# Holding back two pairs of weight loads with copies of one column

## The chip, the cores and the metric

The kernel runs on one core of a Trainium2 chip. The metric is device time in microseconds (us), the median of the runs of one kernel; lower is better. Engine names are those of the profile: PE is TensorE (PEld its weight loads), DVE is VectorE, ACT is ScalarE, POOL is GpSimd, SP is SyncE, which here only issues DMAs. ACT and POOL issue DMAs too. A name with q (SPq, ACTq, POOLq) is the engine's sequencer.

## The reference

One decoder block on x of 1024 tokens by 1024 channels, all in float32:

```python
h = _rmsnorm(x, g_mix_pre)
u_pool, q, k, v, gates = split(h @ w_in + b_in)
y_pool = _multiscale_pool(u_pool, w_pool, pool_scale)      # windows 2, 4, 8, 16; 4 groups of 128
y_attn = _sliding_window_sink_attention(rotary(q), rotary(k), v, sinks)
g_pool, g_attn = split(sigmoid(gates))
merged = g_pool * (y_pool @ w_branch_pool) + g_attn * (y_attn @ w_branch_attn)
x = x + _rmsnorm(merged @ w_out, g_mix_post)
h2 = _rmsnorm(x, g_mlp_pre)
x = x + _rmsnorm(square(relu(h2 @ w_up)) @ w_down, g_mlp_post)
```

The change concerns w_out alone, more exactly when parts of it are fetched from HBM.

## The kernel before

Every product runs on PE as three passes of a reduced-precision type: each operand is split into a high part (a cast on ACT, line L101) and a low part (a subtraction on DVE, L104), and high times high, high times low and low times high are summed. The big products (gates, w_out, w_up, w_down) use Strassen's scheme with seven block products, so they need sums and differences of quarter blocks as operands. For w_out the quarter blocks are W_Q[a, b], each 512 rows by 512 columns, held as two tiles of 512 KB.

The work goes in stages: attention with the pooled inputs woven in, the gates (`gt`, lines L494 to L535), the two branches, the output product (L1027), then w_up and w_down. The gates end by storing 16 sigmoid tiles z to HBM (L693, issued by ACT, queue ACTq). The change lies in the branches:

- Attention branches 0 to 7 (`branch(w_ba[m], ..., 8, m)`), 24 matmuls each on PE (L428, L430). At every even m, `gate_pair` loads the stored gates of two branches as two tiles `zg[8, m // 2]` (L905, 512 KB each, tiles named g); the branch's weights are loaded (L418, tile st) and split into wh (L101, L104); the result, in two PSUM banks mm, is multiplied into the gates on DVE (L916). There are four such banks, so branch m + 2 may begin only when the products L916 of branch m are done.
- `pool_part(gi)` prepares one group of the pooled mixer during branches 2, 3, 5 and 6, groups 1, 0, 2, 3 in this order. It loads d (L920, SP), adds a bias (ACT, L671), sums over the window by doubling (DVE, L675 and L676, into tiles t), finishes d (L679 to L681) and splits it into yphi (ACT) and yplo (DVE). Tiles d, t and the last z of the gates share four buffers of one pool, tag y: the first d waits until a z store has landed.
- Pooled branches 0 to 7 (`branch(wbp_dram[m], ..., 0, m)`) do the same with the group results and the gates `zg[0, m // 2]`.

Along the way the sums of quarter blocks that the output product wants are made by DMA: `wo_load` loads one block (SP), and `wo_add` adds another one to it while it is read (POOL, a DMA that accumulates, `accum_op`). There are two such tile pairs: `sums` (two ga buffers, in the profile s<-in_w_o_dram) and `s3` (two bc buffers).

```python
    def wo_load(quad, place):
        ts = [place([2, 512]) for _ in range(2)]
        for j, t in enumerate(ts):
            nc.sync.dma_start(t, W_Q[quad][2 * j:2 * j + 2].rearrange("k p n -> p k n"))   # L941
        return ts
...
    for m in range(8):
        branch(w_ba[m], lambda k, hl, th: asp[th][k // 2][hl][:, k % 2, :], 8, m)
        if m == 4:
            sums = wo_load((1, 0), a32)
            wo_add(sums, (1, 1))                                                          # L946
```

`sums` is first read in pooled branch 2 (`split_pairs(sums, x_place)`, tiles wo<-s), then gets block (0, 0) added, later (0, 1). `s3` is read only in the output product. Their place in the code is not their place in time. From the branches on the code is outside of the hand-ordered section; a scheduler orders the instructions of each engine, and a load whose buffer is free early is put early. Each engine, and SP's and POOL's queue of DMA issues, then works strictly in its order: an instruction that waits holds up all behind it.

Of the kernel before, what the change touches and what calls it, by code (L numbers as in the profile page):

```python
# [50 lines left out]
def block_kernel(ctx: ExitStack, tc, xt, x, consts, vecs, sinks, b_qkv, g_post, g_mlp_post,  # L51
                 w_qkv, w_u, w_g, w_pool, w_bp, w_ba, w_o, w_up, w_dn, x1_dram, spill, y_dram, wbp_dram, f_dram, out):
    nc = tc.nc
    act, dve, pool, pe = nc.scalar, nc.vector, nc.gpsimd, nc.tensor
# [32 lines left out]
    def bank(tag, shape=None):  # L87
        return psum["pool"].tile([P] + (shape or [512]), F32, tag=tag, name=nm(tag), bufs=psum["bufs"][tag])
# [327 lines left out]
    def load_w(src, shape):  # L416
        ws = stage(shape)
        nc.sync.dma_start(ws, src)  # L418
        hi, lo = wslot(shape), wslot(shape)
        split(hi, lo, ws)  # L420
        return hi, lo

    def mm_fm(bs, whi, wlo, rhs, nk):

        for k in range(nk):
            for th in range(2):
                for hl in range(2):
                    pe.matmul(bs[th], whi[:, k, :], rhs(k, hl, th), start=k == 0 and hl == 0, stop=False)  # L428
            for th in range(2):
                pe.matmul(bs[th], wlo[:, k, :], rhs(k, 0, th), start=False, stop=k == nk - 1)  # L430
# [469 lines left out]
    zg = {}  # L900

    def gate_pair(base, j):
        zg[base, j] = [g32([2, 512]) for _ in range(2)]
        for th, t in enumerate(zg[base, j]):
            nc.sync.dma_start(t, z_dram[base + 2 * j:base + 2 * j + 2, :, th * 512:(th + 1) * 512]  # L905
                              .rearrange("m p n -> p m n"))

    def branch(w, rhs, base, m):
        if m % 2 == 0:
            gate_pair(base, m // 2)  # L910
        z = zg[base, m // 2]
        whi, wlo = load_w(w, [4, P])
        bs = [bank("mm"), bank("mm")]
        mm_fm(bs, whi, wlo, rhs, 4)
        for th in range(2):
            dve.tensor_tensor(z[th][:, m % 2], z[th][:, m % 2], bs[th], ALU.mult)  # L916

    def pool_part(gi):
        u = yy.tile([P, S], F32, tag="y", name=nm("d"))
        nc.sync.dma_start(u, u_dram[gi])  # L920
        for _ in pool_in(gi, u, y_place):
            pass
        hi = xp.tile([P, S], F32R, tag="x", name=nm("yphi"))
        lo = xp.tile([P, S], F32R, tag="x", name=nm("yplo"))
        split(hi, lo, u)
        ysp[gi] = hi, lo
# [3 lines left out]
    def split_pairs(srcs, place):  # L930
        ops = [(place([2, 512]), place([2, 512])) for _ in srcs]
        for (hi, lo), t in zip(ops, srcs):
            split(hi, lo, t)
        return ops

    W_Q = {(a, b): w_o[4 * b:4 * b + 4, :, 512 * a:512 * a + 512] for a in range(2) for b in range(2)}

    def wo_load(quad, place):
        ts = [place([2, 512]) for _ in range(2)]
        for j, t in enumerate(ts):  # L940
            nc.sync.dma_start(t, W_Q[quad][2 * j:2 * j + 2].rearrange("k p n -> p k n"))  # L941
        return ts

    def wo_add(ts, quad):
        for j, t in enumerate(ts):
            pool.dma_start(t, W_Q[quad][2 * j:2 * j + 2].rearrange("k p n -> p k n"), accum_op=ALU.add)  # L946
# [8 lines left out]
    for m in range(8):  # L955
        branch(w_ba[m], lambda k, hl, th: asp[th][k // 2][hl][:, k % 2, :], 8, m)
        if m == 4:
            sums = wo_load((1, 0), a32)
            wo_add(sums, (1, 1))
        if m in (2, 3, 5, 6):  # L960
            pool_part({2: 1, 3: 0, 5: 2, 6: 3}[m])

    def merge(j):
        for z, zp in zip(zg[8, j], zg.pop((0, j))):
            dve.tensor_tensor(z, z, zp, ALU.add)
# [7 lines left out]
    b11, b12 = merged(0, 1), merged(0, 0)  # L973
    for m in range(8):
        branch(wbp_dram[m], lambda k, hl, th: ysp[k][hl][:, th * 512:(th + 1) * 512], 0, m)
        if m % 2:
            merge(m // 2)
        if m == 0:
            wop[1] = split_pairs(wo_load((0, 0), stage), x_place)
            s3 = wo_load((1, 0), bc32)  # L980
            wo_add(s3, (0, 0))
        elif m == 2:
            wop[5] = split_pairs(sums, x_place)
            wo_add(sums, (0, 0))
        elif m in (4, 6):
            j = m // 2 - 2
            gop.setdefault(1, []).extend(split_pairs(b11[j:j + 1], gr))
            dve.tensor_tensor(b11[j], b11[j], b12[j], ALU.subtract)
# [554 lines left out]
```

## Time and profile before

| what | us |
|---|---|
| median of 3 runs | 1117.25 (1117.24, 1117.25, 1119.76) |
| the profiled execution's own time | 1119.41 |
| its span, first to last instruction | 1117.6 |
| PE busy in the span | 1101.0 |
| DVE, ACT, POOL busy | 807.0, 549.5, 54.9 |
| attention branch 0 begins on PE | 320.50 |
| pooled branch 0 begins on PE | 372.04 |
| output product begins on PE | 415.56 |

A timeline row is: start, duration, engine, line, operation, out<-in, shapes, count, and in brackets the idle time of the engine before it with what ended it. Start times count from the span's start. A row of waits is: who waited, for whom, total us, times, longest. In the profile a tile's buffer numbers are left out.

### The profile page before, as it was taken

Reading aid. Unit: us, or ns where it says so; the run is one execution under the profiler, and the core shown is the slowest. Engines: PE = TensorE matmul, PEld = TensorE weight load, DVE = VectorE, ACT = ScalarE, POOL = GpSimd, SP = SyncE. Lnnn points to the kernel's source line nnn. Section 1 sums busy time; section 2 is a strip of 40 time slices with the busy share of each in tenths; the row PEclk is TensorE's granted clock in tenths of the full one; section 3 lists DMA queues with packets and bytes.
Section 4 is the critical chain, followed back from the end, with each engine's and each line's share of the span. In section 5 each row is a group of like instructions: output and inputs, shape, how many; then the busy total and the mean of one; then the engine's idle time right before and its main releaser. Section 6 shows DMA issues by size and latency. Waiting matters only on the chain.

```text
span 1117.6 us, 13863 instructions
## 1 busy us (share of the span) xinstructions
PE 1101.0 (99%) x5119; PEld 909.8 (81%) x5119; DVE 807.0 (72%) x1174; ACT 549.5 (49%) x917; POOL 54.9 (5%) x101
## 2 busy tenths in 40 slices
PE   9999999999998999999999999999999999999997
PEld 7888788888876888888888888888888888888885
DVE  5478867899747896899988866666548944456596
ACT  7466656445422326677545545454444434344342
POOL 0333221000000000000000000000000000000000
PEclk9999999999999999999999999999999999999999
DMA  9305569456787532481357655435697635335672
GB/s 353 133 11 137 147 152 312 148 188 207 262 248 257 138 95 74 141 287 47 130 209 264 242 188 173 176 125 208 214 362 251 205 96 175 104 97 159 197 251 108
DMA packets 88420, 203.19 MB, mean 182 GB/s; under 512 B 7328, under 2 KB 19744, under 8 KB 88352
## 3 DMA queue, kind: packets, MB, share of 16 engines
q1 hardware_dynamic: 76208, 176.35, 47.1%
q10 hardware_dynamic: 5616, 19.66, 4.5%
q0 software_dynamic: 6528, 6.29, 4.0%
q8 instruction: 40, 0.66, 0.2%
q14 instruction: 28, 0.23, 0.1%
HBM read 146.70 MB, written 55.57 MB: 181 GB/s over the span
## 4 chain that ended last, share of the span: by engine, by line
PE 89%; DVE 4%; DMA 4%; ACT 2%; issue 1%; SPq 0%; DVEq 0%; ACTq 0%
PE mm L494 24%; PE at L494 16%; PE at L1385 14%; PE mm L1385 12%; PE mm L428 4%; PE at L1027 4%; PE mm L1027 3%; PE mm L187 3%; PE mm L584 2%; PE mm L430 2%; DMA spill_dram<-z 1%; PE at L196 1%; PE sc L187 1%; PE at L399 1%; DMA g<-spill_dram 1%; PE sc L335 1%
## 5 line engine op out<-in xcount | busy, mean ns | idle before, releaser
L1385 PE MATMUL at<-ar,wh 128*128 128x512 f32 x744 | 169.9, 389 | 0.3 <-DVE ar L104 0.3
L1385 PEld LDWEIGHTS at<-ar,wh 128*128 128x128 f32 x744 | 139.5, 188 | 30.0 <-DVE ar L104 0.7
L104 DVE TENSOR_TENSOR wh<-raw,wh 128x1024 fp32r<-128x1024 f32 x53 | 64.8, 1223 | 97.6 <-ACT wh L101 97.6
L1385 PE MATMUL mm<-ar,wh 128*128 128x512 f32 x576 | 131.0, 389 | 0.0
L101 ACT CAST wh<-raw 128x1024 fp32r<-128x1024 f32 x53 | 55.8, 1053 | 146.1 <-PE at L1385 65.2
L1385 PEld LDWEIGHTS mm<-ar,wh 128*128 128x128 f32 x576 | 108.1, 188 | 22.4
L101 ACT CAST wh<-st 128x512 fp32r<-128x512 f32 (+1 forms) x97 | 61.5, 645 | 65.3 <-PE at L494 19.9
L104 DVE TENSOR_TENSOR wh<-st,wh 128x512 fp32r<-128x512 f32 (+1 forms) x97 | 68.9, 720 | 25.1 <-ACT wh L101 22.7
L494 PE MATMUL mm<-gr,wh 128*128 128x512 f32 x333 | 80.2, 391 | 0.0
L494 PEld LDWEIGHTS mm<-gr,wh 128*128 128x128 f32 x333 | 62.1, 188 | 12.8
L494 PE MATMUL mm<-T,wx 128*128 128x512 f32 x288 | 67.5, 389 | 0.0
L494 PEld LDWEIGHTS mm<-T,wx 128*128 128x128 f32 x288 | 54.1, 188 | 11.2
L494 PE MATMUL at<-T,wx 128*128 128x512 f32 x252 | 59.1, 389 | 0.0
L494 PEld LDWEIGHTS at<-T,wx 128*128 128x128 f32 x252 | 47.3, 188 | 9.8
L494 PE MATMUL mm<-x,wh 128*128 128x512 f32 x240 | 55.2, 389 | 0.0
L494 PEld LDWEIGHTS mm<-x,wh 128*128 128x128 f32 x240 | 45.0, 188 | 9.4
L104 DVE TENSOR_TENSOR ar<-B,ar 128x1024 fp32r<-128x1024 f32 x37 | 45.1, 1220 | 4.2 <-ACT ar L101 4.0
L584 PE MATMUL mm<-x,wh 128*128 128x512 f32 x192 | 47.8, 396 | 0.0
L101 ACT CAST ar<-B 128x1024 fp32r<-128x1024 f32 x37 | 38.9, 1051 | 6.3 <-DMA B<-in_w_dn_dram 3.4
L584 PEld LDWEIGHTS mm<-x,wh 128*128 128x128 f32 x192 | 35.2, 188 | 7.7
L494 PE MATMUL at<-gr,wh 128*128 128x512 f32 x150 | 36.6, 390 | 0.0
L101 ACT CAST wx<-ws 128x512 fp32r<-128x512 f32 x30 | 18.6, 620 | 33.0 <-DVE ws L470 17.9
(386 smaller groups left out, 2160.5 us busy)
## 6 DMA issues: line engine op xcount, KB each, us to landing
raw<-f_dram SPq DMA_DIRECT2D x53, 512.0 KB, 3.7
f_dram<-g SPq DMA_DIRECT2D x30, 512.0 KB, 3.3
B<-in_w_dn_dram SPq DMA_DIRECT2D x24, 512.0 KB, 6.6
st<-in_w_up_dram SPq DMA_DIRECT2D x20, 512.0 KB, 3.8
st<-in_w_g_dram SPq DMA_DIRECT2D x18, 512.0 KB, 4.3
f_dram<-g ACTq DMA_DIRECT2D x17, 512.0 KB, 2.8
g<-spill_dram SPq DMA_DIRECT2D x16, 512.0 KB, 7.2
raw<-in_w_dn_dram SPq DMA_DIRECT2D x16, 512.0 KB, 4.6
```

The costliest lines, as they stand in the source:

```text
L101: act.copy(hi, src)
L104: eng.tensor_tensor(lo, src, f32(hi), ALU.subtract)
L187: pe.matmul(bq, xs_[k][n // 4][:, xh, n % 4 * P:(n % 4 + 1) * P], wq[k][:, h, :], start=k == 0 and j == 0, stop=k == NK - 1 and j == 2)
L196: pe.matmul(bkv_of(n), xs_[k][n // 4][:, xh, n % 4 * P:(n % 4 + 1) * P], wkv[k // 2][:, h, k % 2, :], start=k == 0 and j == 0 and not (joi ...
L335: pe.matmul(sb[:, kv, i, :nk], qt[r, qx, m * P:(m + 1) * P], kx[r, k0:k0 + nk], start=j == 0, stop=j == 2)
L399: pe.matmul(flat(yb), v[:, kv, :], flat(p[:, 4 * kv:4 * kv + 4]), start=j == 0, stop=j == len(mms) - 1)
L428: pe.matmul(bs[th], whi[:, k, :], rhs(k, hl, th), start=k == 0 and hl == 0, stop=False)
L430: pe.matmul(bs[th], wlo[:, k, :], rhs(k, 0, th), start=False, stop=k == nk - 1)
L494: pe.matmul(b, w[:, wh, kt, :], xo[kt][:, xh, :], start=not after and kt == 0 and j == 0, stop=kt == 3 and j == 2, skip_group_check=after)
L584: pe.matmul(b, (whi, wlo)[h][:, k, :], xr(k, xh, th), start=j == 0, stop=j == len(mms) - 1)
L1027: pe.matmul(bs[t], gop[i][kt // 2][gh][:, kt % 2, t * P:(t + 1) * P], wop[i][kt // 2][wh][:, kt % 2], start=not after and kt == 0 and j == ...
L1385: pe.matmul(bs[t], fo[fh][:, k2, t * P:(t + 1) * P], wo_[wh][:, k2, :], start=not after and s2 == 0 and k2 == 0 and j == 0, stop=s2 == NS ...
```

## The change

`wo_load` may be given a tile `behind`. It then first copies one column of it into each new tile on POOL. The load that overwrites the tile must wait for the copy, and the copy waits for what wrote `behind`: here the product L916 of a branch into its second gate tile. `sums` is held so behind attention branch 4, `s3` behind pooled branch 1, which also moves the code of `s3` by one branch. The copied values are overwritten by the loads.

```diff
-    def wo_load(quad, place):
+    def wo_load(quad, place, behind=None):
         ts = [place([2, 512]) for _ in range(2)]
+        for t in ts if behind else ():
+            pool.tensor_copy(t[:, 0, :1], behind[:, 0, :1])
         for j, t in enumerate(ts):
             nc.sync.dma_start(t, W_Q[quad][2 * j:2 * j + 2].rearrange("k p n -> p k n"))
...
         if m == 4:
-            sums = wo_load((1, 0), a32)
+            sums = wo_load((1, 0), a32, zg[8, 2][1])
             wo_add(sums, (1, 1))
...
         branch(wbp_dram[m], lambda k, hl, th: ysp[k][hl][:, th * 512:(th + 1) * 512], 0, m)
+        if m == 1:
+            s3 = wo_load((1, 0), bc32, zg[0, 0][1])
+            wo_add(s3, (0, 0))
         if m % 2:
             merge(m // 2)
         if m == 0:
             wop[1] = split_pairs(wo_load((0, 0), stage), x_place)
-            s3 = wo_load((1, 0), bc32)
-            wo_add(s3, (0, 0))
```

PE, DVE and ACT keep their instructions in the same order; SP and POOL change. On SP, in the stretch of the attention branches, before (st are branch weights, g stored gates, d the pooled groups; s_528 and s_529 are `sums`, s_574 is the second tile of `s3`, whose first tile stood some 30 rows earlier, among the gates' weights):

```order
L418 DMA st_3261<-in_w_ba_dram 128x512
L941 DMA s_528_3346<-in_w_o_dram 128x2x512
L941 DMA s_529_3347<-in_w_o_dram 128x2x512
L905 DMA g_3207<-spill_dram 128x2x512
L905 DMA g_3208<-spill_dram 128x2x512
L418 DMA st_3312<-in_w_ba_dram 128x512
L920 DMA d_3245<-spill_dram 128x1024
L905 DMA g_3308<-spill_dram 128x2x512
L905 DMA g_3309<-spill_dram 128x2x512
L418 DMA st_3352<-in_w_ba_dram 128x512
L941 DMA s_574_3550<-in_w_o_dram 128x2x512
L920 DMA d_3295<-spill_dram 128x1024
```

The same place on SP after:

```order
L418 DMA st_3261<-in_w_ba_dram 128x512
L905 DMA g_3207<-spill_dram 128x2x512
L905 DMA g_3208<-spill_dram 128x2x512
L418 DMA st_3312<-in_w_ba_dram 128x512
L920 DMA d_3245<-spill_dram 128x1024
L905 DMA g_3308<-spill_dram 128x2x512
L905 DMA g_3309<-spill_dram 128x2x512
L418 DMA st_3354<-in_w_ba_dram 128x512
L920 DMA d_3295<-spill_dram 128x1024
```

The three loads of sums are gone from between the gates and the pooled groups; the rest keeps its order. On SP at the pooled branches, after, `sums` now stands between the two tiles of block (0, 0) (st_3539 and st_3540, loaded at pooled branch 0), ahead of the weights of pooled branch 1 (st_3551):

```order
L418 DMA st_3505<-wbp_dram 128x512
L905 DMA g_3680<-spill_dram 128x2x512
L943 DMA st_3539<-in_w_o_dram 128x2x512
L943 DMA s_528_3346<-in_w_o_dram 128x2x512
L943 DMA s_529_3347<-in_w_o_dram 128x2x512
L943 DMA st_3540<-in_w_o_dram 128x2x512
L418 DMA st_3551<-wbp_dram 128x512
```

Before, the two loads s_528 and s_529 were missing there. `s3` (s_578, s_579) moved likewise, to behind the weights of pooled branch 5 and ahead of those of branches 6 and 7. On POOL, from the last of the attention's issues on, before:

```order
L404 DMA y_dram<-yt_1901 256x1x128 x2
L946 DMA s_573_3549<-in_w_o_dram 128x2x512
L946 DMA s_528_3346<-in_w_o_dram 128x2x512
L946 DMA s_529_3347<-in_w_o_dram 128x2x512
L946 DMA s_574_3550<-in_w_o_dram 128x2x512
```

and after:

```order
L404 DMA y_dram<-yt_1901 256x1x128 x2
L941 COPY s_528_3346<-g_3309 128x1
L941 COPY s_529_3347<-g_3309 128x1
L948 DMA s_528_3346<-in_w_o_dram 128x2x512
L948 DMA s_529_3347<-in_w_o_dram 128x2x512
```

The copies stand ahead of the first additions to `sums`. The second additions to `sums` follow in both; only behind them come, after the change, the copies for `s3` and its two additions, which before stood around the first additions to `sums`; the third additions to `sums` are last in both.

## The prediction

> **What bounds the kernel now.** I read the waits of PE first, then PE's timeline where they fall, then back along the engines to what each wait stood on. PE's waits over the whole run (all others are 1.5 us or less and lie elsewhere):
>
> ```profile
> PE mm L428 <- ACT wh L101: 4.0, 1, 4.0
> PE mm L428 <- DVE g L916: 1.7, 1, 1.7
> ```
>
> Both are in the attention branches. PE's timeline there (rows of one branch's first matmul, but for the fifth), and the clock in a window of 4 us (PE, PEld, DVE, ACT and POOL busy, granted clock, DMA share, GB/s):
>
> ```profile
> 320.50 0.39 PE L428 MATMUL mm<-yahi,wh 128*128 128x512 f32 x1
> 333.22 0.47 PE L428 MATMUL mm<-yahi,wh 128*128 128x512 f32 x1 [1.68 <-DVE g L916]
> 348.50 0.47 PE L428 MATMUL mm<-yahi,wh 128*128 128x512 f32 x1 [4.03 <-ACT wh L101]
> 349.04 0.63 PE L428 MATMUL mm<-yahi,wh 128*128 128x512 f32 x1
> 355.71 0.39 PE L428 MATMUL mm<-yahi,wh 128*128 128x512 f32 x1
> 361.15 0.39 PE L428 MATMUL mm<-yahi,wh 128*128 128x512 f32 x1
> 372.04 0.39 PE L428 MATMUL mm<-yphi,wh 128*128 128x512 f32 x1
> ...
> 348.00:352.00 4.00, 3.50 (x9) 2.65 (x10) 3.97 (x7) 0.47 (x1) 0.00 (x0) 0.65 0.80 293
> ```
>
> A branch that waits for nothing takes 361.15 - 355.71 = 5.44. Branches 0 to 4 took 355.71 - 320.50 = 35.21 instead of 27.20: 8.01 us are lost here. Of these branch 2 (due at 320.50 + 2 x 5.44 = 331.38, begun at 333.22) cost 1.84, branch 4 (due 5.44 + 5.44 after 333.22, so 344.10, begun at 348.50) 4.4 with what branches 2 and 3 ran over, and branch 4 itself 355.71 - 348.50 - 5.44 = 1.77, since its matmuls ran at a granted clock of 0.65.
>
> What the waits stood on, DVE and ACT around them:
>
> ```profile
> 317.77 2.88 PE L494 MATMUL mm<-x,wh 128*128 128x512 f32 x12
> 320.63 1.15 ACT L671 ACTIVATE d<-d,vec 128x1024 f32<-128x1024 f32 x1 [10.46 <-DMA d<-spill_dram]
> 321.81 1.23 DVE L675 TENSOR_TENSOR t<-d 128x1023 f32<-128x1023 f32 x1 [5.87 <-ACT d L671]
> 322.96 0.68 DVE L529 TENSOR_TENSOR z<-z,mm 128x512 f32<-128x512 f32 x1
> 326.12 0.35 ACTq L693 DMA_DIRECT2D spill_dram<-z  x1
> 329.99 1.23 DVE L675 TENSOR_TENSOR t<-t 128x1022 f32<-128x1022 f32 x1 [3.29 <-DMA spill_dram<-z]
> 332.39 1.28 DVE L916 TENSOR_TENSOR g<-g,mm 128x512 f32<-128x512 f32 x2
> 334.26 0.15 DVE L681 TENSOR_TENSOR d<-t,d 128x3 f32<-128x3 f32 x1
> 335.11 0.87 SPq L920 DMA_DIRECT2D d<-spill_dram  x1
> 345.35 1.15 ACT L671 ACTIVATE d<-d,vec 128x1024 f32<-128x1024 f32 x1 [8.29 <-DMA d<-spill_dram]
> 346.53 1.23 DVE L675 TENSOR_TENSOR t<-d 128x1023 f32<-128x1023 f32 x1 [5.51 <-ACT d L671]
> 347.67 1.28 DVE L916 TENSOR_TENSOR g<-g,mm 128x512 f32<-128x512 f32 x2
> ```
>
> DVE sits idle for 5.87 and 5.51 us, because the next instruction in its order belongs to a pooled group whose d is not there, and the products L916 that free PE's banks stand behind it. 332.39 is branch 0's product (PE goes on at 333.22), 347.67 is branch 2's (PE goes on at 348.50; the row names ACT, whose last cast ended there as well, but that cast is of a later branch's weights). So the first cause is two late loads of d. The chain of waits and the DMA view say why they are late:
>
> ```profile
> 307.54 9.18 DMA spill_dram<-z
> 316.79 3.82 DMA d<-spill_dram
> 327.92 5.69 DMA spill_dram<-z
> ...
> DMA to landing us min/median/max: 10.2/10.2/10.2
> ...
> spill_dram<-z ACTq DMA_DIRECT2D x14, 512.0 KB, 3.9
> ```
>
> The first d waits for a z store that took 9.18 where the median of 14 such is 3.9; the d issued at 335.11 took 10.2 (the row of that one issue). What else was moving: the queues between 299 and 343 us (packets, MB, share of 16 engines) with the three accumulating issues, and then those of 308 to 312:
>
> ```profile
> q1 hardware_dynamic: 3445, 7.20, 50.7%
> q0 software_dynamic: 816, 1.57, 20.5%
> s<-in_w_o_dram POOLq DMA_DIRECT2D x3, 512.0 KB, 9.5
> ...
> q0 software_dynamic: 198, 0.40, 60.9%
> q10 hardware_dynamic: 3, 0.01, 0.8%
> ```
>
> Three accumulations of 0.52 MB fill all 16 engines for 0.205 x 44 = 9.0 us, 3.0 each; a plain 0.52 MB on q1 takes 0.507 x 44 x 0.524 / 7.20 = 1.6. In 308 to 312 the accumulation (q0) has 60.9% and ACT's queue (q10), where the z store waits, 0.8%.
>
> **The change part by part.**
>
> 1. It takes three plain loads and three accumulations of sums out of 299 to 343: 3 x 1.6 + 3 x 3.0 = 14 of 44 us of DMA time. The earliest load and accumulation of s3, among the gates, go too; PE waits for nothing there, so nothing comes of it.
>
> 2. The z store of 307.54 then lands after 3.9 (the median; at most 9.18 as now). From 311.4: d 3.8, ACT 1.2, so DVE has its L675 at 316.5 and is done at 317.7, ahead of L529, which PE frees at 317.97 (0.2 after the next group begins at 317.77). L529 comes 5.0 earlier than its 322.96, and with it the store of 326.12, now 321.1. The last store hangs on PE's last gate group (320.5) and comes some 4 earlier, 323.9.
>
> 3. DVE's next L675 waited for the store of 326.12 to land, 3.87 after its issue; now at 321.1 + 3.9 = 325.0, again 5.0 earlier. Branch 0's product then runs from 327.4 to 328.7. PE wants it at 331.38, so the first wait goes, with 2.7 to spare.
>
> 4. L681 ends at 329.3. SP reaches the next d once the last store has landed, at 323.9 + 5.7 = 329.6 at the latest (it took 5.69), so at about 330 instead of 335.11. Its landing lies between 3.8 (the first d) and 10.2; I take 5.5, since two gate loads of 1.6 stand ahead of it and no accumulation. Then 335.5, ACT until 336.7, DVE's L675 until 338, branch 2's product behind it, its first half done at 338.7. PE wants it at 320.50 + 4 x 5.44 = 342.26. Even at 10.2 the half is done at 343.4, and 1.2 of the 4.4 is left. So the second wait goes, and the slow stretch with it.
>
> 5. What is added: four copies on POOL, priced by POOL's nearest row, 0.29 each, and waits. The sums come later, and this is the place to look for a new wait:
>
> ```profile
> 359.60 1.28 DVE L916 TENSOR_TENSOR g<-g,mm 128x512 f32<-128x512 f32 x2
> 374.89 1.05 ACT L101 CAST wo<-s 128x1024 fp32r<-128x1024 f32 x1
> 377.90 1.28 DVE L916 TENSOR_TENSOR g<-g,mm 128x512 f32<-128x512 f32 x2
> L305 POOL COPY vf<-qkv x6: 290/295/444, 40.3 to 94.9; 128x128 f32<-128x128 f32 x6
> st<-in_w_o_dram SPq DMA_DIRECT2D x6, 512.0 KB, 3.8
> DMA to landing us min/median/max: 5.6/5.7/6.1
> ...
> s<-in_w_o_dram SPq DMA_DIRECT2D x3, 512.0 KB, 6.1
> DMA to landing us min/median/max: 10.3/10.3/10.3
> ```
>
> Branch 4's product is the row of 359.60; 8.0 earlier it ends at 352.9, the copies at 353.5. The loads land after 3.8 (the median of the same block's plain loads), 357.8 with the second a little behind. The accumulations land after 5.7 (the row of the four after 356 us, when little else moves; the last two rows are the crowd's, the three loads of sums between 299 and 343 and the first accumulation), and POOL issues the second when the first has landed, so 363.5 and 369.5. ACT casts the second sum at 374.89, now due at 366.9: it waits 2.6 there, until 370.6. Behind it on DVE stand its low part, 1.2, and pooled branch 0's product (377.90), first half done at 372.5. PE wants that at 372.04 - 8.0 + 2 x 5.44 = 374.9. Cost 0, with 2.4 to spare; gone when the pair of accumulations takes 2.4 longer.
>
> 6. On SP, the loads of sums wait for the copies until 353.5. Behind them stand the second tile of block (0, 0) and the weights of pooled branch 1, whose buffers DVE frees about then or later. Cost 0. The loads of s3 wait for copies that stand on POOL behind the second additions (issued after 370.6 and one landing later), so until about 378; behind them on SP are the weights of pooled branches 6 and 7. Branch 6 begins on PE at 364.0 + 6 x 5.44 = 396.7, so its weights have over 15 us. s3 itself is read in the output product, over 40 us later. Cost 0.
>
> The sum: -8.0, so the profiled execution of 1119.41 becomes 1111.4. It stands 2.16 over the median of 1117.25. If that is the price of profiling, the median becomes 1109.2. If its waits or its slow stretch were longer than in the median run, the time without them is 1111.4 for every run. The runs themselves lie 2.5 apart (1117.24 and 1119.76), about the size of the slow stretch, and the rest of the kernel is PE at its pace; so I take a value nearer the second, 1111.0.
>
> The Trainium skill (TensorE: Matmul & The Clock Gate, Part 1: The HAM clock gate) says that an idle stretch of about 3.4 us, counted in windows that run freely, halves PE's clock for a while, and that the outcome varies from run to run. By that rule a remnant of 1.2 would bring no slow stretch, and the three runs may differ by it. The trace agrees: 4.03 idle was followed by a clock of 0.65, 1.68 was not.
>
> **The rivals.**
>
> - B, even sharing. The store was slow because three queues shared the engines, and the accumulation held it up only by its share. A third of the engines would give the store 3 x 1.6 + 2.3 = 7.1 (2.3 is 3.9 less 1.6), half of them 5.5, a gain of 1.6 and not 5.3. Then every step up to branch 0's product comes 1.7 earlier (330.7 to 332.0, about 0.3 of PE's wait left), d goes out at 333.4, lands after 7 (10.2 less one accumulation), and branch 2's product is done at 343.5, 1.2 late. 1111.0 + 1.5 = 1112.5. Against it: 0.8% for q10 beside 60.9% for q0. The Trainium skill (DMA: Bandwidth & Descriptors, Queues, rings and completion order) speaks for it: each DMA engine goes round its queues packet by packet. The rows of 308 to 312 do not look like that.
> - C, late sums, on the other side. The loads and the accumulations of sums take as long as in the crowd: 6.1 and twice 10.3. The second sum lands at 353.5 + 6.1 + 10.3 + 0.3 + 10.3 = 380.5, the product's first half is done 3.0 later, pooled branch 2 waits 8.6 and then runs slowly for 1.8: 1111.0 + 10.4 = 1121.4. It decides when the pair needs over 14 instead of 11.7. Against it: 5.6 to 6.1 for the four accumulations after 356.
> - D, nothing comes of it for the second wait: the gate loads that SP sends in a row make the second d as late as now, and only the first wait goes: 1111.0 + 4.4 + 1.8 = 1117.2, or 2.0 below the median, 1115.2. Against it: accumulations and loads of sums are 14 of the 39 us that the engines were busy between 299 and 343.
>
> **How the numbers follow.** A, as worked out, 0.70, from 1109.2 to 1111.4 with a small remnant; B 0.16; C 0.07; D 0.07. About 0.3%, 3.4 us, is what can be told from no change: faster is under 1113.9. A and nearly all of B are there, 0.84; D and a little of B are the same, 0.09; slower is C, 0.07. The range leaves C and D out and reaches from A's lower end to over B: 1109.0 to 1114.0.
>
> **What would show it.** Right: PE has no wait over 0.5 at L428 and the granted clock stays at 1.00 from 344 to 352; the z store of 307.5 lands within 5, ACT's d L671 comes at about 316 and 336; L916 of branch 0 stands before 329; the span is near 1109.6. Wrong: ACT's wo<-s shows an idle time of over 5 that ends by the DMA of s, with PE waiting at pooled branch 2 (C); DVE's L675 still waits over 3 for ACT's d near 340 (B, D).

## The result, and the profile after

The changed kernel takes 1112.08 us in the median of 6 runs (1110.14 to 1114.83). The kernel before, run beside it, took 1118.71 (1117.24 to 1123.13). The ratio is 0.9938, with a 95% interval of 0.9915 to 0.9961: about 6.9 us faster by the ratio, 6.6 by the medians; the forecast was 6.2, from 1117.25 to 1111.0. The profiled execution took 1114.83 (span 1113.1), against 1119.41 (span 1117.6).

PE's waits in the branches, after (the columns are total, times, longest):

```profile
PE mm L428 <- DVE g L916: 2.0, 1, 2.0
```

PE's timeline, the first matmul of attention branches 2 and 4 and of pooled branches 0, 1 and 2:

```profile
331.58 0.39 PE L428 MATMUL mm<-yahi,wh 128*128 128x512 f32 x1
342.46 0.39 PE L428 MATMUL mm<-yahi,wh 128*128 128x512 f32 x1
364.22 0.39 PE L428 MATMUL mm<-yphi,wh 128*128 128x512 f32 x1
369.81 0.47 PE L428 MATMUL mm<-yphi,wh 128*128 128x512 f32 x1
377.63 0.47 PE L428 MATMUL mm<-yphi,wh 128*128 128x512 f32 x1 [2.04 <-DVE g L916]
```

The first branch begins at 320.70, so branches 2 and 4 begin exactly when they are due (320.70 + 2 x 5.44 and + 4 x 5.44). Both old waits are gone, and so is the slow stretch: the window that showed a granted clock of 0.65 now shows 1.00 (the third number from the end).

```profile
348.00:352.00 4.00, 4.00 (x20) 3.30 (x19) 2.98 (x4) 2.44 (x3) 0.00 (x0) 1.00 0.68 240
```

The attention branches take 364.22 - 320.70 = 43.52, which is 8 x 5.44; before they took 51.54. That is the whole 8.0 of the forecast. But there is a new wait. Pooled branch 1 is 0.15 late, and pooled branch 2, due at 369.81 + 5.44 = 375.25, begins at 377.63. The pooled branches take 46.24 instead of 43.52. So 8.02 are won and 2.72 lost again; the start of the branches (0.21 later) and the rest of the kernel (0.5 longer, with a new 0.8 of waiting at L1388) make the span 4.55 shorter in this pair of executions.

The z store that took 9.18 before, issue and landing, after:

```profile
L693 ACTq DMA_DIRECT2D spill_dram<-z x1: 327/327/327, 307.7 to 307.7; - x1
...
DMA to landing us min/median/max: 2.8/2.8/2.8
```

The rows that answer to those of the late d before: ACT's biases (L671) for the two d loads that were late, and DVE behind them:

```profile
315.37 1.15 ACT L671 ACTIVATE d<-d,vec 128x1024 f32<-128x1024 f32 x1 [4.99 <-DMA d<-spill_dram]
316.56 1.23 DVE L675 TENSOR_TENSOR t<-d 128x1023 f32<-128x1023 f32 x1 [0.41 <-ACT d L671]
326.61 1.28 DVE L916 TENSOR_TENSOR g<-g,mm 128x512 f32<-128x512 f32 x2
336.20 1.16 ACT L671 ACTIVATE d<-d,vec 128x1024 f32<-128x1024 f32 x1 [4.25 <-DMA g<-spill_dram]
338.53 1.28 DVE L916 TENSOR_TENSOR g<-g,mm 128x512 f32<-128x512 f32 x2
```

DVE waits 0.41 for the first d instead of 5.87. (The row of 336.20 names a gate load as the last to come; the second d itself landed at 336.18.) Branch 0's product stands at 326.61 (before at 332.39), branch 2's at 338.53 (before at 347.67), nearly 4 us before PE wants it, at 342.46.

And the rows of the new wait, on POOL (the first additions to `sums`), ACT (the cast of the second tile), DVE (its low part and pooled branch 0's product):

```profile
352.69 1.72 POOL L941 COPY s<-g 128x1 f32<-128x1 f32 x2 [172.35 <-DVE t L676]
357.58 1.24 POOL L948 DMA_DIRECT2D s<-in_w_o_dram  x1 [3.17 <-DMA s<-in_w_o_dram]
366.17 1.22 POOL L948 DMA_DIRECT2D s<-in_w_o_dram  x1 [7.35 <-DMA s<-in_w_o_dram]
374.58 1.05 ACT L101 CAST wo<-s 128x1024 fp32r<-128x1024 f32 x1 [4.96 <-DMA s<-in_w_o_dram]
375.66 1.23 DVE L104 TENSOR_TENSOR wo<-s,wo 128x1024 fp32r<-128x1024 f32 x1 [3.66 <-ACT wo L101]
376.81 1.28 DVE L916 TENSOR_TENSOR g<-g,mm 128x512 f32<-128x512 f32 x2
```

Read from below: PE waits for the product of 376.81; that stands on DVE behind the low part of the second sum; that waits for ACT's cast; the cast waits 4.96 for the second addition, issued at 366.17 and landed at 374.48. Both additions took 8.3, where the forecast had 5.7. (The copies' row names L676 before them; what they have to wait for is the product L916, which stands on DVE just ahead of it.)

### The profile page after: what moved, and what is told of

Read it like the earlier page. It is cut to its first block, busy times and chain, and to the rows that moved or that the text cites. A ratio compares the mean times of both kernels' runs of the same rounds, so it can differ in the third digit from the quotient of the medians.

```text
span 1113.1 us, 13873 instructions
## 1 busy us (share of the span) xinstructions
PE 1099.7 (99%) x5119; PEld 908.8 (82%) x5119; DVE 807.0 (73%) x1174; ACT 549.8 (49%) x917; POOL 57.3 (5%) x105
## 4 chain that ended last, share of the span: by engine, by line
PE 86%; DVE 6%; DMA 4%; ACT 2%; issue 1%; SPq 0%; POOL 0%; DVEq 0%; POOLq 0%; ACTq 0%
PE mm L494 24%; PE at L494 16%; PE at L1388 14%; PE mm L1388 12%; PE at L1030 4%; PE mm L1030 3%; PE mm L187 3%; PE mm L584 2%; PE mm L428 2%; DMA s<-in_w_o_dram 1%; PE at L196 1%; PE mm L430 1%; PE sc L187 1%; PE at L399 1%; DMA g<-spill_dram 1%
## 5 line engine op out<-in xcount | busy, mean ns | idle before, releaser
L1388 PE MATMUL at<-ar,wh 128*128 128x512 f32 x744 | 169.9, 389 | 1.1 <-ACT ar L101 0.8
L1388 PEld LDWEIGHTS at<-ar,wh 128*128 128x128 f32 x744 | 139.5, 188 | 30.8 <-ACT ar L101 1.2
L104 DVE TENSOR_TENSOR wh<-raw,wh 128x1024 fp32r<-128x1024 f32 x53 | 64.8, 1223 | 97.8 <-ACT wh L101 97.8
L1388 PE MATMUL mm<-ar,wh 128*128 128x512 f32 x576 | 131.0, 389 | 0.0
L1388 PEld LDWEIGHTS mm<-ar,wh 128*128 128x128 f32 x576 | 108.1, 188 | 22.4
L104 DVE TENSOR_TENSOR wh<-st,wh 128x512 fp32r<-128x512 f32 (+1 forms) x97 | 69.0, 720 | 27.7 <-ACT wh L101 25.4
L104 DVE TENSOR_TENSOR ar<-B,ar 128x1024 fp32r<-128x1024 f32 x37 | 45.1, 1220 | 4.4 <-ACT ar L101 4.3
```

Of the source, the lines that this page charges most:

```text
L104: eng.tensor_tensor(lo, src, f32(hi), ALU.subtract)
L1388: pe.matmul(bs[t], fo[fh][:, k2, t * P:(t + 1) * P], wo_[wh][:, k2, :], start=not after and s2 == 0 and k2 == 0 and j == 0, stop=s2 == NS ...
```

## The experiments

Branch lengths are read from one profiled execution of each kernel; without any wait the attention and the pooled branches take 43.52 each. "z store" is the store issued near 307.5, from issue to landing. Ratios are to the kernel before on the same chip.

| kernel | z store | attention branches | pooled branches | median, ratio [interval] |
|---|---|---|---|---|
| before | 9.18 | 51.54 | 43.52 | |
| after | 2.79 | 43.52 | 46.24 | 1112.08, 0.9938 [0.9915, 0.9961] |
| e1 only sums held | 2.77 | 45.39 | 46.37 | 1115.43, 0.9972 [0.9956, 0.9988] |
| e2 only s3 held | 9.10 | 46.67 | 43.52 | 1113.88, 0.9954 [0.9938, 0.9971] |
| e3 sums behind branch 3 | 2.89 | 43.52 | 43.52 | 1111.56, 0.9934 [0.9918, 0.9950] |
| e4 sums behind branch 5 | 2.79 | 43.52 | 47.01 | 1115.50, 0.9968 [0.9955, 0.9981] |
| e5 no early additions | 4.55 | 43.52 | 43.52 | 1111.14, 0.9943 [0.9925, 0.9962] |
| e6 plain loads on POOL | 9.25 | 52.72 | 43.52 | 1117.98, 0.9994 [0.9980, 1.0008] |
| e7 after, again | 2.79 | 43.66 | 45.33 | 1112.98, 0.9949 [0.9936, 0.9962] |
| e8 as e3, again | 2.78 | 43.52 | 43.52 | 1111.08, 0.9938 [0.9924, 0.9952] |
| e9 plain loads on SP | 8.32 | 47.94 | 43.52 | 1115.47, 0.9964 [0.9953, 0.9976] |
| e10 one plain load on POOL | 8.10 | 46.48 | 43.52 | 1113.40, 0.9951 [0.9934, 0.9967] |
| e11 one addition | 8.59 | 47.51 | 43.52 | 1115.13, 0.9966 [0.9953, 0.9979] |
| e12 one plain load on SP | 7.03 | 45.98 | 43.52 | 1113.96, 0.9960 [0.9942, 0.9979] |

**Which half of the change removes which wait.** e1 keeps only the hold of `sums`:

```diff
-        if m == 1:
-            s3 = wo_load((1, 0), bc32, zg[0, 0][1])
-            wo_add(s3, (0, 0))
...
         if m == 0:
             wop[1] = split_pairs(wo_load((0, 0), stage), x_place)
+            s3 = wo_load((1, 0), bc32)
+            wo_add(s3, (0, 0))
```

> Only sums is held, behind attention branch 4; s3 is loaded and added to as in the kernel before (one of its two additions beside the first gates, the other near 333 us). Theory A (each addition takes about 3.0 us of all 16 DMA engines and holds up what stands beside it, so the additions to sums made the z store late and the one to s3 helped to make the second d late): the first wait (1.8) is gone, the second d lands in 7.2 + 3.0 = 10.2 after about 329, so near 339.3, and branch 2's product is done at about 342.3, on time within 0.5; the 2.0 at pooled branch 2 stays. Median 1112 to 1113. Rival (the addition to s3 alone makes the second wait): the 4.4 and the slow clock are back, 1117 to 1118.

e2 keeps only the hold of `s3`:

```diff
-            sums = wo_load((1, 0), a32, zg[8, 2][1])
+            sums = wo_load((1, 0), a32)
```

> Only s3 is held, behind pooled branch 1; sums is loaded and added to as in the kernel before. Theory A: the z store of 307.5 still takes 9 and PE still waits 1.7 at branch 2; the second d, without the addition beside it, lands in 5.6 to 7.2 instead of 10.2, so the wait of 4.0 shrinks to 0 to 1.2 and the slow clock goes; no wait at pooled branch 2, since sums has landed long before. Median 1111.5 to 1113.5. Rival (the late d of 335 is only a consequence of the late z store, the addition beside it does not matter): both waits as before, 1117.

The d load of about 330 (or 335), from issue to landing, in e1 and then in e2:

```profile
L920 SPq DMA_DIRECT2D d<-spill_dram x1: 983/983/983, 329.6 to 329.6; - x1
...
DMA to landing us min/median/max: 10.3/10.3/10.3
```

```profile
L920 SPq DMA_DIRECT2D d<-spill_dram x1: 384/384/384, 334.6 to 334.6; - x1
DMA to landing us min/median/max: 6.6/6.6/6.6
```

Both landings came as theory A had them, 10.3 with the addition to `s3` just ahead and 6.6 without. In e1 the first wait is gone, and the late d costs 0.75 at branch 4 and 0.75 more at branch 6, which the expectation had missed; the attention branches lose 1.87. The pooled branches lose 2.85, but not where the expectation had it: 1.88 at pooled branch 1 and 0.75 at pooled branch 2. At pooled branch 1 ACT waits for that branch's weight:

```profile
368.52 0.62 ACT L101 CAST wh<-st 128x512 fp32r<-128x512 f32 x1 [4.47 <-DMA st<-wbp_dram]
```

The weight was issued at 361.52, beside the first addition to `sums`, and took 6.92; the kernel before has it land after 2.72.

In e2 the z store is late as before and costs 1.9 at branch 2, while branch 4 is only 0.35 late: 3.15 lost. The losses do not add up to the 8.02 of before, since each hold alone already takes away most of the long wait at branch 4: that wait needs a late start (the z store) and a slow d (the addition to `s3`) together. By these waits the rivals in both expectations fall. The medians missed their ranges: 1115.43 is 2.4 above e1's, 1113.88 is 0.4 above e2's.

**Where sums should be held.** e3 holds it one branch earlier, e4 one later:

```diff
-        if m == 4:
-            sums = wo_load((1, 0), a32, zg[8, 2][1])
+        if m == 3:                                              # e3
+            sums = wo_load((1, 0), a32, zg[8, 1][1][:, 1:])     # e3
+        if m == 5:                                              # e4
+            sums = wo_load((1, 0), a32, zg[8, 2][1][:, 1:])     # e4
             wo_add(sums, (1, 1))
```

> As the changed kernel, but sums is held behind attention branch 3, one branch earlier. If the 2.0 at pooled branch 2 comes from the late landing of the second addition, the pair lands 5 earlier, at about 369, the wait and the 0.7 beside it go, and pooled branches take 43.5 instead of 46.2: median 1112.1 - 2.7 = 1109.4. Rival (the additions are slow wherever they stand and now hold up the last d, issued at 343): a new wait of 1 to 2 at attention branches 5 to 7, median 1111 to 1112.

> As the changed kernel, but sums is held behind attention branch 5, one branch later. If the landing of the pair sets pooled branch 2 one to one, the wait of 2.0 grows by a branch's 5.4 to 7.4, and the granted clock falls after it for 1.8: median 1112.1 + 5.4 to 7.2 = 1117.5 to 1119.3, as slow as the kernel before. Rival (the additions took 8.3 only because of the loads beside them, and go in 5.7 each when later): the wait grows to 2 to 3 only, median 1112 to 1114.

In e3 PE waits nowhere in the branches, and both halves take 43.52. Its median, 1111.56, is 2.2 above the expected 1109.4, though, and hardly below the 1112.08 of the changed kernel, which was not measured beside it; e7 and e8 below put the two together. In e4 the wait at pooled branch 2 grows, but by 1.1 and not by a branch. Its wait and its two additions:

```profile
PE mm L428 <- DVE g L916: 3.1, 1, 3.1
```

```profile
L948 POOL DMA_DIRECT2D s<-in_w_o_dram x1: 1237/1237/1237, 362.8 to 362.8; - x1
...
DMA to landing us min/median/max: 6.0/6.0/6.0
```

```profile
L948 POOL DMA_DIRECT2D s<-in_w_o_dram x1: 1219/1219/1219, 369.1 to 369.1; - x1
...
DMA to landing us min/median/max: 6.1/6.1/6.1
```

The first addition went out 5.25 later than in the changed kernel (362.83 for 357.58), but the pair landed only 0.7 later (375.18 for 374.48), since each addition took 6.0 instead of 8.3. So the rival's mechanism fits e4: the additions are faster where less runs beside them. SP's queue moved 0.51 and 0.60 MB while e4's two were under way, 1.03 and 1.02 MB while those of the changed kernel were. In the changed kernel the second tile of `sums`, a tile of block (0, 0) and a pooled weight (issued at 354.44, 354.90 and 358.80) ran beside the first addition, and four weights (366.47 to 370.89), issued after it, beside the second. No run changes this traffic alone, and it is not all: in e7 an addition took 7.1 with 0.6 MB beside it. The granted clock stayed at 1.00 behind e4's wait of 3.1, as behind the 2.0 of the changed kernel. The end follows the landing one to one: 0.7 later, and the pooled branches 0.77 longer. The median of 1115.5 lies between the two expectations: 2.1 to 3.4 over the changed kernel by the ratios (0.9968 less 0.9949 or 0.9938), where the branches explain 0.8 to 1.5. What the rest is stays open.

e7 and e8 put the changed kernel and e3 side by side on one chip.

> The changed kernel once more, beside the others on one chip. Its branches take 89.8 as in its first profile, with 2.0 at pooled branch 2, and the ratio to the kernel before stays at 0.9938: near 1111.5 where before takes 1118.4.

> sums held behind attention branch 3 again, now beside the changed kernel on one chip. If the 2.7 that its branches were shorter (87.04 instead of 89.76) reach the end, its median is 2.7 below the changed kernel's. Rival (the time comes back later, in the output product or w_up, where waits of 0.3 to 1.3 come and go): it is less than 1 below.

1112.98 (1111.61 to 1113.88) against 1111.08 (1110.54 to 1112.96), 1.9 apart; the branches are 88.99 and 87.04 long in these executions, 1.95 apart. The runs overlap and so do the two intervals, so the gain of 1.9 is likely, not certain. It is less than the 2.7 expected because the changed kernel lost only 1.8 in the pooled branches this time (1.08 of it at pooled branch 1, whose weight took 6.12 to land). In e8 the second sum is there when ACT comes to it, without a wait:

```profile
367.59 1.05 ACT L101 CAST wo<-s 128x1024 fp32r<-128x1024 f32 x1
```

**What made the z store late.** The prediction blamed the accumulation. e5 is the kernel before without its four early additions:

```diff
             sums = wo_load((1, 0), a32)
-            wo_add(sums, (1, 1))
...
             s3 = wo_load((1, 0), bc32)
-            wo_add(s3, (0, 0))
```

> The kernel before with its plain loads of sums and s3 where they were, but without the four additions that stood early (two to sums, two to s3), so these sums hold one block less. Theory A (the additions make the z store and the second d late, the plain loads hardly): the z store of 307.5 lands within 5, both waits at L428 are under 0.5, and the branches take 87.0 to 87.6 instead of 95.06: median 1109 to 1111. Rival B (even sharing; loads count as additions do): the z store takes 5.5 to 7, a wait of 0.3 or more at branch 2 and of 1 or more at branch 4 stay: median 1112 to 1114.

e6 and e9 put plain loads of the same blocks in their place, on POOL and on SP:

```diff
+    def wo_put(ts, quad):
+        for j, t in enumerate(ts):
+            pool.dma_start(t, W_Q[quad][2 * j:2 * j + 2].rearrange("k p n -> p k n"))   # e9: nc.sync
...
-            wo_add(sums, (1, 1))
+            wo_put(sums, (1, 1))
...
-            wo_add(s3, (0, 0))
+            wo_put(s3, (0, 0))
```

> The kernel before with its four early additions turned into plain loads of the same blocks, issued by POOL at the same places, so these sums hold one block only. If it is the adding that is costly (3.0 us of all engines for 0.52 MB where a plain load takes 1.6): q0 takes half the engine time and the z store lands in 4 to 6, the first wait under 0.5, the second under 1: median 1110 to 1112. If it is POOL's queue, whatever it carries, that gets ahead of ACT's: the z store takes 7 to 9 and at least the first wait of 1.7 stays: median 1113 to 1117.

> As with plain loads on POOL (the four early additions turned into plain loads, sums hold one block only), but SP issues these loads. Theory 'POOL's queue': the bytes are the same, but the z store of 307.5 has its first packets within 1 to 2 us of its issue and lands within 6; the first wait is under 0.7; median 1110 to 1113. Rival 'bytes': the store takes 7 to 9 as on POOL, the first wait of 1.7 stays, median 1115 to 1118.

Theory A passes e5: no wait at all with the plain loads of sums where they were. But e6 speaks against the adding as the cause. Plain loads on POOL delay the store as much (9.25), though each takes 1.3 of engine time (22.0% of 16 engines for 12 us, for two of them) against 3.1 for an addition. Two of them stand ahead of the store there, where the kernel before has one addition; e10 and e11 below have one of each. The second d, issued at 334.21 in e6, is as slow as before too, 10.9, behind POOL's plain load of 332.13. And e9 shows that it does not take POOL's queue either. (e6's median of 1117.98 is 1.0 above its expected range.) The queues in 308 to 312 (packets, MB, share of the 16 engines), first in e9, then in the changed kernel, where of all these loads only the two gate loads of 303 stand ahead of the store:

```profile
q1 hardware_dynamic: 646, 1.26, 99.0%
q10 hardware_dynamic: 1, 0.00, 0.2%
```

```profile
q10 hardware_dynamic: 205, 0.77, 56.0%
q1 hardware_dynamic: 149, 0.26, 19.6%
```

In e9 the store was issued at 307.38 and had 0.2% of the engines until 312, while SP's queue, whose loads were issued at 304.2 to 306.0, had 99.0%. The picture is that of the kernel before (60.9% and 0.8%) with another queue in the first place. It does not last: from 312 to 316 both queues of e9 move at once, ACT's (q10) with this z store and the next:

```profile
q10 hardware_dynamic: 280, 1.02, 63.2%
q1 hardware_dynamic: 212, 0.37, 25.4%
```

So the transfers issued ahead of the store decide when it begins; once it moves, it shares the engines with what is left of them.

The last three put a single transfer of 0.52 MB ahead of the store (into the first tile of `sums`, `wo_put(sums[:1], (1, 1))` or `wo_add(sums[:1], (1, 1))`; no other early addition):

> The kernel before with a single early plain load of 0.52 MB on POOL (into the first tile of sums, in the place of its first addition) and without the other three early additions; the sums lack these blocks. 'POOL's queue': the z store's first packets come 3.5 to 4.5 after its issue, after POOL's, and it lands after 7 to 9; the first wait of about 1.7 stays, the second mostly goes (no addition near 333): median 1113 to 1115. 'Adding': the load takes half the engine time of an addition, the store lands within 6, the first wait is under 0.5: median 1110 to 1112.

> The same with a single early addition (into the first tile of sums) instead of the plain load; the other three are left out, so the sums lack these blocks. By both theories the z store takes about 9 and the first wait of 1.7 to 1.8 stays, since this addition is the one beside the store; the second wait mostly goes: median 1113 to 1115. If the store lands within 6, it is the second addition or the sum of them that counts, and the reading of the shares was wrong: median 1110 to 1112.

> As with one early plain load on POOL, but SP issues it, so the same 0.52 MB stand ahead of the z store in another queue; the sums lack the other blocks. So far the z store took 4.55 with none, 8.10 with one on POOL, 8.32 with two on SP. If it is the bytes ahead, whoever issues them: half way between none and two on SP, 6.4, and POOL's 8.10 has 1.7 of its own; the first wait is 0 to 0.2, the branches take 87.0 to 87.5, median 1111 to 1112. If a single load ahead is enough whoever issues it: 8, a first wait of 0.4 and branches of 89 to 90 as with one on POOL, median 1113 to 1114.

The store's landing in e5 (no transfer added ahead), e12 (one plain load on SP), e9 (two on SP) and e11 (one addition), in this order:

```profile
L693 ACTq DMA_DIRECT2D spill_dram<-z x1: 326/326/326, 307.0 to 307.0; - x1
...
DMA to landing us min/median/max: 4.6/4.6/4.6
```

```profile
L693 ACTq DMA_DIRECT2D spill_dram<-z x1: 326/326/326, 307.3 to 307.3; - x1
...
DMA to landing us min/median/max: 7.0/7.0/7.0
```

```profile
L693 ACTq DMA_DIRECT2D spill_dram<-z x1: 326/326/326, 307.4 to 307.4; - x1
...
DMA to landing us min/median/max: 8.3/8.3/8.3
```

```profile
L693 ACTq DMA_DIRECT2D spill_dram<-z x1: 327/327/327, 307.3 to 307.3; - x1
...
DMA to landing us min/median/max: 8.6/8.6/8.6
```

The row's first numbers are the issue itself, the last line the landing. No, one and two added loads on SP give 4.6, 7.0 and 8.3, so the store waits for what was issued ahead of it, but not in proportion: the first load costs 2.5 and the second 1.3. Even e5's 4.55 is not free of this. Its two loads of `sums`, issued at 298.43 and 299.41, delay the gate loads behind them, and the changed kernel, without them, has 2.79. Of the 9.18 before, 1.8 thus come with the plain loads of `sums`, which theory A had put at hardly anything, and about 4 with one addition (e11).

One plain load on POOL gives 8.1, 1.1 more than on SP, and the addition 0.5 more than that, though its packets take 1.7 times as long (24.5% against 14.1% of the engines from 305 to 317). Why POOL's load costs 1.1 more than SP's is open, from one execution of each.

e12's 7.0 lies between its two expectations (6.4 and 8); its first wait, its branches (89.5) and its median are those of the second, which let a single load be enough. Branch 2 begins only 0.3 late in e10, 0.4 in e12, 0.9 in e9 and 1.0 in e11, where the expectations of e10 and e11 and e9's rival had a wait of 1.7: it follows the landing of the first d behind the store, at 319.06, 318.79, 319.44 and 319.57, against 320.61 before with 1.8. In e9 and e11 PE waits another 1.6 and 1.5 at branch 6, which no expectation had.

## Why the prediction was right, point by point

The forecast of 1111.0 with 1109.0 to 1114.0 held: 1112.08, and 1112.98 in the second series. Its main case came true in the attention branches and was diluted by a small form of rival C. Of its signs of being right two failed: PE waits 2.0 at L428, and the span is 1113.1, not near 1109.6. That the median came so near is in part luck. The profiled execution was forecast at 1111.4 and took 1114.83, the highest of its six runs; its branches are 5.3 shorter than before, not 8.0, while the medians lie 6.6 apart; and 1111.0 was chosen between 1109.2 and 1111.4.

- Step 1, the transfers taken out: right in what it brings. e5 shows that taking away the four additions alone is enough for the attention branches to run at their pace.
- Step 2, the z store "lands after 3.9": it took 2.79. L675 was forecast for 316.5 and stands at 316.56; the later stores for 321.1 and 323.9, they stand at 321.35 and 324.01. The first d took 4.68 instead of 3.8.
- Step 3, branch 0's product "from 327.4 to 328.7": it stands at 326.61.
- Step 4, the second d issued "at about 330", landing 5.5: issued at 329.03, and its landing took 7.15. The product of branch 2, forecast from 338, stands at 338.53. e1 and e2 show the two causes of the long wait apart.
- Step 5 is the term that was mis-sized. "The accumulations land after 5.7": they took 8.27 and 8.31, 2.6 more each. The additions went out nearly as forecast (357.58 for 357.8), so the pair landed at 374.48 instead of 369.5, 5.0 later. The step had 2.4 to spare and said that the cover is gone beyond that; 5.0 - 2.4 = 2.6, and pooled branch 2 begins 2.4 late. The 5.7 was taken from four additions in a quiet stretch, without counting what runs beside them at their new place, the held loads among it; that this is the reason is argued from e4, not isolated. The copies were mis-sized as well, 0.86 each instead of 0.29, but this cost nothing: the first load goes out behind the first copy.
- Step 6: the loads of `s3` cost nothing, as forecast. The weight of pooled branch 1 did cost something: 0.15 and 1.1 in the two executions of the changed kernel, 1.9 in e1. The loads of sums ahead of it on SP did not hold up its issue (SP waits 3.4 there for DVE's L104). But beside the first addition it took 6.2, 6.1 and 6.9 to land, against 2.7 before.
- The sum: -8.0 for the profiled execution; measured -8.02 in the attention branches and +2.72 in the pooled ones.
- Rival B, 1112.5, is nearer to the measured median than A's 1111.0, but for another reason. Its mechanism, even sharing, falls: in e9 the store, issued at 307.38, got 0.2% of the engines from 308 to 312, where half would have been its share. The Trainium skill (DMA: Bandwidth & Descriptors, Queues, rings and completion order) has each DMA engine go round its queues packet by packet; with that alone, if its packets stood ready, the store would have moved along from its issue, and the trace, 99.0% against 0.2% until 312, does not agree; that both queues move from 312 on does. No run here shows when the packets stood ready. A's reading of the same rows, that the accumulation itself holds the store up, falls with e9 and with e10 beside e11. What is left is what was issued ahead.
- Rival C came in its place and by its mechanism, ACT idle for 4.96 until the sum lands, but with 2.0 instead of 8.6: it decides from a pair of 14 us on, the pair took 16.9 (357.58 to 374.48). Its price was too high since it took 10.3 for each addition, where 8.3 came. Rival D did not come: the second wait is gone.

## What to carry to other kernels

A late transfer may be late by what was issued before it, on whatever queue: look for the prefetches that nobody needs yet and that stand just ahead of a transfer on the path, and hold them until the path's transfers are out. Hold them no longer than that, and price the held transfers by what will run beside them at their new place, themselves included and also what is issued after them. Here one branch earlier is free on both sides (87.04 us for the branches), and the place behind branch 4 cost 1.8 to 2.7. A copy of one column is a cheap way to tie a load to a moment of the program.

## What had not been expected of the hardware

- A copy of a 128x1 column on POOL took 0.86 (1.72 for two), three times the 0.29 of a 128x128 copy earlier in the kernel; DVE was busy beside it.
- Plain transfers of two issuing engines can land in the order of their issue. In e9 those of 304.23, 304.66, 305.17, 306.01 and 307.38 landed at 308.79, 311.11, 312.44, 315.63 and 315.70, the last one from another queue. It is no rule: in e12 the store of 307.29 landed at 314.32, the load of 305.66 at 314.50, and in the changed kernel a weight issued at 366.47 landed at 368.90, the addition of 366.17 only at 374.48.
- An addition of 0.52 MB has its first packet 1.9 us after its issue when little else moves and takes 2.8 to 3.6 of the 16 engines' time, a plain load on POOL 1.3 to 1.7 and once 3.0 (e6, issued at 332.13); yet one of each ahead of the z store made it 8.6 and 8.1, nearly the same.
